# Channel mix by one level of Strassen's algorithm in a two-layer trunk: weight sums by accumulating DMAs, tiles in pools by phase

## The chip, the cores and the metric

The kernel runs on one core of a Trainium2 chip. A core has five engines with a queue each: TensorE (PE; its weight loads are listed apart as PEld), VectorE (DVE), ScalarE (ACT), GpSimd (POOL) and SyncE (SP), which here only issues DMAs. Each engine works through its own queue in order; semaphores tie the queues together. On-chip data lie in SBUF (128 partitions), products in PSUM (8 banks of 128 x 512 float32). The metric is the device time of one execution in microseconds.

## The reference

Two layers over 512 tokens with 1024 features. Cut to what matters (`i` is the layer):

```python
h = rmsnorm(x, norm1_g[i]);  z = h @ w_in[i] + b_in[i]
y_m = sigmoid(mo) * head_layernorm(mlstm(mq, mk, mv, mi, mf))        # 4 heads
y_r = silu(rg) * head_layernorm(retention(rq, rk, rv))               # 4 heads
merged = sigmoid(gm) * (y_m @ w_bm[i]) + sigmoid(gr) * (y_r @ w_br[i])
x = x + merged @ w_out[i]
h2 = rmsnorm(x, norm2_g[i])
x = x + square(relu(h2 @ w_ff1[i] + b_ff1[i])) @ w_ff2[i] + b_ff2[i]   # channel mix, 1024 -> 4096 -> 1024
h3 = rmsnorm(x, norm3_g[i])
x = x + sigmoid(h3 @ w_pe_gate[i]) * (p[i] @ w_pe[i])
return rmsnorm(x, final_g)
```

The change is in the fourth line from the end, the channel mix; it is 2 x 1024 x 4096 weights per layer.

## The kernel before

Activations lie transposed: features on partitions, the 512 tokens on the free axis. So a tile of weights (128 x 128) is the operand that PE holds, and the tokens stream past it. Every float32 operand of PE is split into two parts, `hi` = the value rounded to PE's float32r and `lo` = the rest; a product is the three matmuls hi*hi, hi*lo and lo*hi (`mm3`, lines 196 to 198). A split is two instructions: ACT writes `hi` by a copy, then DVE subtracts it and writes `lo`.

The weights come as one stream of 406 units of 512 KB (203 per layer) in the order of use. A unit of kind T8 holds the weights of 128 output features: 8 tiles for the 8 tiles of input features. `load_unit` issues a unit's DMA on SP's queue into `wr` (4 buffers) and splits it into `wh` (line 183, ACT) and `wl` (line 185, DVE), 3 buffers each; `unit` keeps two units ready beyond the one in use. `t8` then runs the unit's 24 matmuls of 512 tokens into one PSUM bank.

The channel mix takes the 4096 hidden features in four blocks `b` of 1024. For each block, eight `t8` make the hidden features (PSUM tiles `l0f`): DVE multiplies by the norm's reciprocal root, ACT adds the bias and takes the relu, POOL squares (line 747), and ACT and DVE split the result into `hid`. Then eight `t8` multiply `hid` by `w_ff2` (PSUM tiles `l0fo`), and DVE adds each into `x` (lines 777 and 779). The norm's sum of squares over features (`finish`) and the spreading of the reciprocal root over partitions (`spread`) are short matmuls after the first and the second `t8` of block 0; so the first result is held until then.

Ahead of the channel mix stand the out projection (`l0wo`, eight `t8`), which makes the norm's operand tile by tile (`n2.tile`), and behind it the layer's embedding (`l0pe`) and its gate (`l0pg`). At the very end of layer 1 the last four units of the gate are run in two halves of 256 tokens (PSUM tiles `pl`).

What sets the order: the code is written in the order of PE's work, and a scheduler orders each engine's queue from it by what is ready; pools hand out buffers, and a queue waits where a buffer is still read.

Of the kernel before, what the change touches and what calls it, by code (L numbers as in the profile page):

```python
# [22 lines left out]
P = 128  # L23
T = 512
# [6 lines left out]
UN = 1024  # L31
LOOK = 2
LAST = 4

# columns of w_in
# [3 lines left out]
# columns of the per-partition vectors  # L39
# [9 lines left out]

def unit_list():  # L50
    """What each unit of the weight stream holds, in the order of use (one layer)."""
# [48 lines left out]
    full("w_in", CGR)  # L100
# [11 lines left out]
    full("w_br", 0, 1024)  # L112
    full("w_out")
    for b in range(4):
        full("w_ff1", b * 1024)
        full("w_ff2", 0, b * 1024)
    u.append(("PE", 0))
    u.append(("PE", 1))
    full("w_pe_gate")
# [3 lines left out]
def build(ctx, tc, ins, out):  # L123
    nc = tc.nc
    ve, ac, gp, te = nc.vector, nc.scalar, nc.gpsimd, nc.tensor
    units = unit_list()
# [4 lines left out]

    cpool = pool("const", 1)
    wpool = pool("w", 3)
    apool = pool("act", 8)
    bpool = pool("big", 2)
    spool = pool("head", 4)
    tpool = pool("tmp", 7)
    opool = pool("one", 1)
    cols = pool("cols", 2)
    psum = pool("ps", 8, space=bass.MemoryType.PSUM)  # L140

    xs_dram = tc.dram_tile([KT, P, T], F32, name="x_spill")

# [10 lines left out]
    sel = cpool.tile([H, H, P], F32R, name="sel")  # L154
    cos = cpool.tile([P, T], F32, name="cos")
    sin = cpool.tile([P, T], F32, name="sin")
# [4 lines left out]
    def tmp(name, shape=(P, 516)):  # L161
        return tpool.tile(list(shape), F32, name=name, tag="t")

# [1 line left out]
    ready = []  # L165
    nxt = [0]

    def load_unit():
        n = nxt[0]
        if n >= L * NU:  # L170
            return
        nxt[0] += 1
        raw = wpool.tile([P, UN], F32, name=f"wr{n}", tag="wr", bufs=4)
        nc.sync.dma_start(raw, ins["wstream"][n])
        if n >= L * NU - LAST:
            hi = [apool.tile([P, T], F32R, name=f"wh{n}{a}", tag="Ah") for a in range(2)]
            lo = [apool.tile([P, T], F32R, name=f"wl{n}{a}", tag="Al") for a in range(2)]
            for a in range(2):
                split(raw[:, a * T:(a + 1) * T], hi[a], lo[a])
            ready.append((units[n % NU], hi, lo))  # L180
            return
        wh = wpool.tile([P, UN], F32R, name=f"wh{n}", tag="wh")
        ac.activation(wh, raw, AF.Copy)  # L183
        wl = wpool.tile([P, UN], F32R, name=f"wl{n}", tag="wl")
        ve.tensor_sub(wl, raw, wh.bitcast(F32))  # L185
        ready.append((units[n % NU], wh, wl))

    def unit(kind):
        while len(ready) < LOOK + 1 and nxt[0] < L * NU:
            load_unit()  # L190
        u, wh, wl = ready.pop(0)
        assert u[0] == kind, (u, kind)
        return u, wh, wl
# [6 lines left out]
    def t8(act, name):  # L200
        """One tile of columns against the 8 tiles of act: a PSUM tile [128 columns, tokens]."""
        _, wh, wl = unit("T8")
        o = ps(name)
        for k in range(KT):
            s = slice(k * P, (k + 1) * P)
            mm3(o, wh[:, s], wl[:, s], act[0][k], act[1][k], k == 0, k == KT - 1)
        return o

    def split(src, hi_ap, lo_ap):
        ac.activation(hi_ap, src, AF.Copy)  # L210
        ve.tensor_sub(lo_ap, src, hi_ap.bitcast(F32))

    def acts(side, name):
        hi, lo = [], []
        for k in range(KT):
            hi.append(apool.tile([P, T], F32R, name=f"{name}h{k}", tag=f"{side}h"))
            lo.append(apool.tile([P, T], F32R, name=f"{name}l{k}", tag=f"{side}l"))
        return hi, lo

# [1 line left out]
    class Norm:  # L221
        """Of the token tiles j0 .. j1 - 1."""

        def __init__(self, name, side, i, gain, j0=0, j1=NT):
# [3 lines left out]
            self.act = acts(side, name) if side else None  # L228
            self.sum = None
# [13 lines left out]

        def square(self, k, x, pool=False):
            w = self.n * P
            x = x[:, self.s]
            if self.sum is None:
                sq = opool.tile([P, T], F32, name=f"{self.name}sum", tag="bv" if self.s.start else "ssum")[:, :w]
            else:
                sq = tmp(f"{self.name}sq{k}")[:, :w]  # L250
# [24 lines left out]
        def spread(self):  # L275
            n = self.name
            w = self.n * P
            dh = opool.tile([P, 1280], F32R, name=f"{n}dh", tag="ph")[:, :w]
            dl = opool.tile([P, 1280], F32R, name=f"{n}dl", tag="pl")[:, :w]
# [7 lines left out]
            self.b = opool.tile([P, T], F32, name=f"{n}rb", tag="rb" if w == T else "dec")[:, :w]  # L287
# [6 lines left out]
    def rows_split_v(i, h, nm, n_, j, o, rc, bvt, vh, vl):  # L294
        """Token-major values of token tile j from the PSUM tile o: + bias, split, into vh, vl."""
# [15 lines left out]
    def values(i, nm, act, nrm, bv_ap, n_):  # L311
        bvt = opool.tile([P, T], F32, name=f"{nm}bv", tag="bv")
        nc.sync.dma_start(bvt, bv_ap)
        o = [ps(f"{nm}vp{j}") for j in range(NT)]
        for u in range(4):
            _, wh, wl = unit("V")
            for kk in range(2):
                k = 2 * u + kk
                s = slice(kk * T, (kk + 1) * T)
                for j in range(NT):  # L320
                    js = slice(j * P, (j + 1) * P)
                    te.matmul(o[j], act[0][k][:, js], wh[:, s], start=(k == 0), stop=False)
                    te.matmul(o[j], act[0][k][:, js], wl[:, s], start=False, stop=False)
                    te.matmul(o[j], act[1][k][:, js], wh[:, s], start=False, stop=(k == KT - 1))
        vh = [spool.tile([P, 516], F32R, name=f"{nm}vh{j}", tag="vh") for j in range(NT)]
        vl = [spool.tile([P, 516], F32R, name=f"{nm}vl{j}", tag="vl") for j in range(NT)]
# [4 lines left out]
    def scores(nm, qh, ql, kh, kl, decay):  # L331
        """P^T tiles: row tile i (128 keys), columns 128 i .. 511 (queries); times the decay."""
        ph = opool.tile([P, 1280], F32R, name=f"{nm}ph", tag="ph")
        pl = opool.tile([P, 1280], F32R, name=f"{nm}pl", tag="pl")
# [37 lines left out]
    def back(nm, num, v):  # L372
        """Columns tile v of the token-major heads, transposed: a PSUM tile [128 features, tokens]."""
# [103 lines left out]
    for i in range(L):  # L477
# [214 lines left out]
        for c in range(KT):  # L692
            gate_tile(sB, c, "bgr")
# [255 lines left out]
```

## Time and profile before

| | us |
|---|---|
| median of 3 runs (2438.12 to 2438.65) | 2438.5 |
| span of the profiled execution, first to last instruction | 2435.6 |
| PE busy | 2412.0 |
| DVE busy | 1349.9 |
| ACT busy | 928.9 |
| POOL busy | 231.0 |

The page gives no time of the profiled execution beside its span; the runs, which have no profile, are 2.9 us longer than the span (their median), which is what lies around the first and the last instruction. A row of a group reads: line, engine, operation, tile written <- tiles read, shapes, how many; after the bar the busy time in us and the mean duration of one in ns; after the second bar the idle time of the engine just before these instructions and what ended it. In a timeline the first two numbers are start and duration in us. Consecutive matmuls overlap in their durations, so their pace is read from starts.

### The profile page before, as it was taken

The numbers are of one execution on the slowest core, as the hardware profiler recorded it, in microseconds if no ns is written. First come the engines' busy times: TensorE is split into PE (matmuls) and PEld (weight loads), VectorE is DVE, ScalarE is ACT, GpSimd is POOL, SyncE is SP. The second block draws the span as 40 slices with busy tenths as digits, with TensorE's granted clock in tenths as the row PEclk, the third lists the DMA queues.
The fourth block names the chain that finished last, engine by engine and source line by source line (L and its number), as shares of the span: only waits on it lengthen the run. The fifth ranks groups of instructions, "written<-read, shape, count | busy, mean of one in ns | idle before, by whom it ended". The sixth has DMA issues, their size and how long they took to land.

```text
span 2435.6 us, 27773 instructions
## 1 busy us (share of the span) xinstructions
PE 2412.0 (99%) x11068; PEld 2006.5 (82%) x11068; DVE 1349.9 (55%) x1974; ACT 928.9 (38%) x1280; POOL 231.0 (9%) x277
## 2 busy tenths in 40 slices
PE   8999999999999999999999999999999999999997
PEld 6888888888888888888888888888888888888887
DVE  7867534666455434435578665446665554434445
ACT  3756323333233423324547552223323333223343
POOL 4000000000000201102101000000000011101122
PEclk9999999999999999999999999999999999999999
DMA  4222232322223333333322222322322242333331
GB/s 165 91 89 77 87 102 89 95 82 90 92 79 123 102 98 100 97 95 104 126 82 91 89 82 93 101 87 87 96 87 87 81 134 89 100 99 95 95 105 52
DMA packets 69498, 232.30 MB, mean 95 GB/s; under 512 B 7540, under 2 KB 9972, under 8 KB 69368
## 3 DMA queue, kind: packets, MB, share of 16 engines
q1 hardware_dynamic: 64040, 220.95, 29.1%
q10 hardware_dynamic: 5328, 9.57, 1.2%
q8 instruction: 87, 1.43, 0.2%
q14 instruction: 43, 0.35, 0.0%
HBM read 226.30 MB, written 4.19 MB: 95 GB/s over the span
## 4 chain that ended last, share of the span: by engine, by line
PE 98%; DVE 1%; ACT 0%; DVEq 0%; POOL 0%; issue 0%; ACTq 0%
PE l1f L196 2%; PE l1f L198 2%; PE l0f L198 2%; PE l1fo L198 2%; PE l0fo L198 2%; PE l0f L196 2%; PE l0fo L197 2%; PE l0f L197 2%; PE l1fo L197 2%; PE l1fo L196 2%; PE l1f L197 2%; PE l0fo L196 2%; PE l0br L196 1%; PE l1br L196 1%; PE l1br L197 1%; PE l0br L197 1%
## 5 line engine op out<-in xcount | busy, mean ns | idle before, releaser
L183 ACT ACTIVATE wh<-wr 128x1024 fp32r<-128x1024 f32 x402 | 426.4, 1061 | 1105.5 <-issue 210.2
L185 DVE TENSOR_TENSOR wl<-wr,wh 128x1024 fp32r<-128x1024 f32 x402 | 493.3, 1227 | 174.6 <-ACT wh L183 172.6
L196 PE MATMUL l1f<-l1n2h,wh 128*128 128x512 f32 x256 | 99.7, 389 | 0.0
L196 PE MATMUL l0f<-l0n2h,wh 128*128 128x512 f32 x256 | 99.7, 389 | 0.0
L198 PE MATMUL l0f<-l0n2h,wl 128*128 128x512 f32 x256 | 99.6, 389 | 0.0
L198 PE MATMUL l1f<-l1n2h,wl 128*128 128x512 f32 x256 | 99.6, 389 | 0.0
L197 PE MATMUL l0f<-l0n2l,wh 128*128 128x512 f32 x256 | 99.6, 389 | 0.0
L197 PE MATMUL l1f<-l1n2l,wh 128*128 128x512 f32 x256 | 99.6, 389 | 0.0
L747 POOL TENSOR_TENSOR l1ft<-l1ft 128x512 f32<-128x512 f32 x32 | 45.8, 1431 | 255.9 <-ACT l1ft L746 251.8
L747 POOL TENSOR_TENSOR l0ft<-l0ft 128x512 f32<-128x512 f32 x32 | 45.7, 1431 | 255.9 <-ACT l0ft L746 251.8
L197 PEld LDWEIGHTS l0f<-l0n2l,wh 128*128 128x128 f32 x256 | 48.1, 188 | 10.1
L197 PEld LDWEIGHTS l1f<-l1n2l,wh 128*128 128x128 f32 x256 | 48.1, 188 | 10.1
L198 PEld LDWEIGHTS l1f<-l1n2h,wl 128*128 128x128 f32 x256 | 48.1, 188 | 10.0
L198 PEld LDWEIGHTS l0f<-l0n2h,wl 128*128 128x128 f32 x256 | 48.0, 188 | 10.0
L196 PEld LDWEIGHTS l0f<-l0n2h,wh 128*128 128x128 f32 x256 | 48.1, 188 | 9.9
L196 PEld LDWEIGHTS l1f<-l1n2h,wh 128*128 128x128 f32 x256 | 48.1, 188 | 9.9
L779 DVE TENSOR_TENSOR l1x<-l1fo,l1x 128x512 f32<-128x512 f32 x24 | 16.6, 691 | 67.1 <-PE l1fo L198 67.1
L779 DVE TENSOR_TENSOR l0x<-l0fo,l0x 128x512 f32<-128x512 f32 x24 | 16.6, 691 | 66.0 <-PE l0fo L198 66.0
L745 DVE TENSOR_TENSOR l0ft<-l0f,l0n2rb 128x512 f32<-128x512 f32 x32 | 22.0, 691 | 35.7 <-PE l0f L198 35.7
L745 DVE TENSOR_TENSOR l1ft<-l1f,l1n2rb 128x512 f32<-128x512 f32 x32 | 22.0, 691 | 35.6 <-PE l1f L198 35.6
L711 DVE TENSOR_TENSOR l0brt<-l0br,l0sB 128x512 f32<-128x512 f32 x16 | 11.1, 692 | 36.2 <-PE l0br L198 36.2
L711 DVE TENSOR_TENSOR l1brt<-l1br,l1sB 128x512 f32<-128x512 f32 x16 | 11.1, 691 | 36.2 <-PE l1br L198 36.2
(2001 smaller groups left out, 6852.7 us busy)
## 6 DMA issues: line engine op xcount, KB each, us to landing
wr<-wstream SPq DMA_DIRECT2D x406, 512.0 KB, 3.5
x<-xT SPq DMA_DIRECT2D x4, 512.0 KB, 5.9
l0xr<-xT ACTq DMA_DIRECT2D x8, 256.0 KB, 2.5
x_spill<-l0x ACTq DMA_DIRECT2D x8, 256.0 KB, 2.8
l1xr<-x_spill ACTq DMA_DIRECT2D x8, 256.0 KB, 2.6
out<-l1x SPq DMA_DIRECT2D x4, 256.0 KB, 2.6
out<-l1x SPq DMA_DIRECT2D x2, 384.0 KB, 3.9
l0pt<-pT ACTq DMA_DIRECT2D x2, 256.0 KB, 2.7
```

The lines of the kernel that those rows point to most:

```text
L183: ac.activation(wh, raw, AF.Copy)
L185: ve.tensor_sub(wl, raw, wh.bitcast(F32))
L196: te.matmul(o, sh, mh, start=first, stop=False)
L197: te.matmul(o, sh, ml, start=False, stop=False)
L198: te.matmul(o, sl, mh, start=False, stop=last)
L711: ve.tensor_tensor(t[:, :T], o, sB[:, c, :], OP.mult)
L745: ve.tensor_tensor(t[:, :T], o, n2.b, OP.mult)
L747: gp.tensor_tensor(t[:, :T], t[:, :T], t[:, :T], OP.mult)
L779: ve.tensor_tensor(x[:, c, :], o, x[:, c, :], OP.add)
```

## The change

The channel mix is done by one level of Strassen's algorithm (in Winograd's form). Two `t8` units of 256 output features become one unit PAIR: a matrix of 1024 x 256 weights seen as 2 x 2 blocks, B11, B21, B22, B12, each 512 x 128 (256 KB); the tokens are seen as two halves of 256 and the input features as two halves of 512. Seven block products of 12 matmuls with 256 tokens (P1 to P7) take the place of 48 matmuls with 512 tokens. Four of the seven weight operands are sums of blocks. They are made in place: after the split of a raw block, POOL issues a DMA that adds the next block from memory to the raw buffer (`gp.dma_start(..., accum_op=OP.add)`), and the sum is split in turn: B11, then t1 = B11+B12, then t2 = t1+B22, then t4 = t2+B21 out of one buffer, and t3 = B22+B12 out of another. (The signs are put into the sums of the tokens and the evacuations.) On the other side, each pair of feature tiles has four quarters of 256 tokens and four sums of them, made by `pair_operand` (DVE) and split; there are seven operand columns `hi`, `lo` of 256.

All weights now come in blocks of 256 KB; a T8 unit is two of them, each loaded and split by itself (7 buffers of `wr`, `wh`, `wl`; `use` prepares 4 blocks ahead). The order of the 64 pairs (32 per layer) and their products is a list: per layer four pairs of `w_ff1`, then a pair of the next block, four pairs of `w_ff2`, three more of `w_ff1`, and so on; P4 of a pair comes after P1 of the next. The relu's square moves from POOL to ACT. The embedding's product stands ahead of the last four pairs. The gate `gr` is computed at the end of the second branch, the first half of the second branch's product goes to memory (`br_dram`) and back, and tiles live in pools that are opened and released by phase.

```diff
-        raw = wpool.tile([P, UN], F32, name=f"wr{n}", tag="wr", bufs=4)
-        nc.sync.dma_start(raw, ins["wstream"][n])
...
+PRODUCTS = {"P1": ("B11", 0), "P2": ("B21", 2), "P3": ("B22", 6), "P4": ("t4", 1), "P5": ("t1", 4),
+            "P6": ("t2", 5), "P7": ("t3", 3)}
+def pair_schedule(n):
...
+    for i in range(n):
+        out.append((i, "P1"))
+        if i:
+            out.append((i - 1, "P4"))
+        out += [(i, x) for x in ("P5", "P2", "P6", "P3", "P7")]
+def prep_schedule(n):
...
+    for i in range(n):
+        out += [(i, "B11"), (i, "B22")]
+        if i:
+            out.append((i - 1, "t4"))
+        out += [(i, x) for x in ("t1", "B21", "t2", "t3")]
...
+    def prep_next():
...
+        raw = raws[n, q]
+        split(raw, wh, wl)
+        pieces[n, x] = wh, wl
+        more = {"B11": 3, "B22": 3, "t1": 2, "t2": 1}.get(x)
+        if more is not None:
+            gp.dma_start(raw, block(n, more), accum_op=OP.add)
...
+        def product(self, x):
...
+            for k in range(4):
...
+                te.matmul(o, wh[:, s], h[:, m], start=f, stop=False, skip_group_check=True)
+                te.matmul(o, wh[:, s], l[:, m], start=False, stop=False, skip_group_check=True)
+                te.matmul(o, wl[:, s], h[:, m], start=False, stop=e, skip_group_check=True)
+            self.done(x, o)
+    def pair_operand(name, st, hi, lo):
+        ve.tensor_tensor(v[:, 4:6, :], v[:, 1:3, :], v[:, 0:1, :].to_broadcast([P, 2, S]), OP.subtract)
+        ve.scalar_tensor_tensor(v[:, 6, :], v[:, 5, :], -1.0, v[:, 1, :], OP.mult, OP.subtract)
+        ve.scalar_tensor_tensor(v[:, 7, :], v[:, 6, :], -1.0, v[:, 3, :], OP.mult, OP.subtract)
+        split(st[:, 4 * S:8 * S], hi[:, 3 * S:7 * S], lo[:, 3 * S:7 * S])
...
+                    if x_ in ("P1", "P5", "P6"):
+                        keep[x_] = small(nm + x_)
+                        ac.activation(keep[x_], o, AF.Copy)
+                    elif x_ == "P2":
+                        ve.tensor_tensor(v[:, 1, :], o, keep["P1"], OP.add)
+                        ve.tensor_tensor(v[:, 1, :], v[:, 1, :], n2.b[:, S:], OP.mult)
+                        act(1, 2, 0, 1.0)
+                    elif x_ == "P3":
+                        ve.tensor_tensor(v[:, 3, :], o, keep["P6"], OP.add)
+                    elif x_ == "P7":
+                        ve.tensor_tensor(v[:, 2, :], o, keep["P5"], OP.add)
+                        ve.tensor_tensor(st[:, 2 * S:4 * S], st[:, 2 * S:4 * S], n2.b, OP.mult)
+                        act(2, 4, 1, -1.0)
+                        pair_quarters(st, *hid[b, p])
+                    elif x_ == "P4":
+                        ve.tensor_tensor(v[:, 0, :], o, n2.b[:, :S], OP.mult)
+                        act(0, 1, 0, 1.0)
+                        pair_operand(nm, st, *hid[b, p])
```

Three places in the engines' queues. First, ACT in a stretch of `w_ff2` before: one split per `t8` and nothing else (`wh141` is the hi part of unit 141).

```order
L183 ACTIVATE wh139_6657<-wr139_6655 128x1024
L746 ACTIVATE l0ft07_6649<-l0ft07_6649,bc_85 128x512
L210 ACTIVATE l0h0h7_6329<-l0ft07_6649 128x512
L183 ACTIVATE wh140_6689<-wr140_6687 128x1024
L183 ACTIVATE wh141_6721<-wr141_6719 128x1024
```

And ACT in such a stretch now (`wh135_t2` is the hi part of t2 of pair 135, `wr135_0` the raw buffer in which B11, t1, t2, t4 of that pair are made one after the other):

```order
L225 ACTIVATE wh135_t2_8087<-wr135_0_7748 128x512
L225 ACTIVATE wh135_t3_8105<-wr135_2_7795 128x512
L225 ACTIVATE wh136_B11_8125<-wr136_0_7901 128x512
L225 ACTIVATE wh136_B22_8144<-wr136_2_7946 128x512
L225 ACTIVATE wh135_t4_8162<-wr135_0_7748 128x512
L225 ACTIVATE wh136_t1_8181<-wr136_0_7901 128x512
L225 ACTIVATE wh136_B21_8199<-wr136_1_7991 128x512
L225 ACTIVATE wh136_t2_8219<-wr136_0_7901 128x512
```

Seven splits of half the width stand there per pair, and those of t1, t2, t4 read a buffer that was split two to four places earlier in the same queue.

Second, DVE in a stretch of `w_ff1` now, from the subtraction for t2 of pair 133 to that for t1 of pair 134 (`l0f03st` and `l0f10st` are the staging tiles of two pairs' hidden features, `l0hl03` the lo part made from one):

```order
L226 TENSOR_TENSOR wl133_t2_7798<-wr133_0_7442,wh133_t2_7797 128x512
L945 TENSOR_TENSOR l0f10st_7775<-l0f10b_7848,l0f10P1_7793 128x256
L226 TENSOR_TENSOR l0hl03_7772<-l0f03st_7622,l0hh03_7771 128x768
L226 TENSOR_TENSOR wl133_t3_7823<-wr133_2_7489,wh133_t3_7822 128x512
L362 TENSOR_TENSOR l0f03st_7622<-l0f03st_7622 128x512
L226 TENSOR_TENSOR wl134_B11_7844<-wr134_0_7595,wh134_B11_7843 128x512
L363 SCALAR_TENSOR_TENSOR l0f03st_7622<-l0f03st_7622 128x256
L946 TENSOR_TENSOR l0f10st_7775<-l0f10st_7775,l0n2rb_7225 128x256
L364 SCALAR_TENSOR_TENSOR l0f03st_7622<-l0f03st_7622 128x256
L226 TENSOR_TENSOR wl134_B22_7866<-wr134_2_7642,wh134_B22_7865 128x512
L226 TENSOR_TENSOR wl133_t4_7885<-wr133_0_7442,wh133_t4_7884 128x512
```

Between the splits of two weight blocks stand the evacuations of products and the sums and splits of the hidden features; before, a stretch of `w_ff1` had one weight split, one multiplication and one split of 512 per `t8`.

Third, POOL, which before squared the hidden features:

```order
L747 TENSOR_TENSOR l0ft00_6421<-l0ft00_6421 128x512
L747 TENSOR_TENSOR l0ft01_6427<-l0ft01_6427 128x512
L747 TENSOR_TENSOR l0ft02_6464<-l0ft02_6464 128x512
```

and which now issues four accumulating DMAs per pair:

```order
L280 DMA wr135_0_7748<-wstream 128x512
L280 DMA wr135_2_7795<-wstream 128x512
L280 DMA wr135_0_7748<-wstream 128x512 x2
L280 DMA wr136_0_7901<-wstream 128x512
L280 DMA wr136_2_7946<-wstream 128x512
L280 DMA wr136_0_7901<-wstream 128x512 x2
```

The rows of one raw buffer (`wr135_0`) are the three additions of a pair that follow on one another; each waits for the DVE subtraction of the split before it.

More of the change, by code (lines that the diff above doesn't have):

```diff
@@ L111, in unit_list, with pairs @@
     rg(3)
-    full("w_br", 0, 1024)
+    for c in range(8):
+        t8("w_in", CGR + c * P)
+        t8("w_br", c * P, 1024)
     full("w_out")
-    for b in range(4):
-        full("w_ff1", b * 1024)
-        full("w_ff2", 0, b * 1024)
+    def pairs(seq):
+        for kind, b, p in seq:
+            if kind == "f":
+                u.append(("PAIR", "w_ff1", 0, b * 1024 + 256 * p))
+            else:
+                u.append(("PAIR", "w_ff2", b * 1024, 256 * p))
+    pairs(ff_order()[0])
     u.append(("PE", 0))
     u.append(("PE", 1))
+    pairs(ff_order()[1])
     full("w_pe_gate")
@@ L188, in unit, with tmp, split @@
-    def unit(kind):
[L189 to L193, printed above, removed]
+    def tmp(name, shape=(P, 516), dt=F32):
+        return cur["tmp"].tile(list(shape), dt, name=name, tag="t", bufs=cur["ntmp"])
+    def split(src, hi_ap, lo_ap):
+        ac.activation(hi_ap, src, AF.Copy)
+        ve.tensor_sub(lo_ap, src, hi_ap.bitcast(F32))
+    use_order, prep_order, loads = [], [], []
@@ new lines, in build, with block, load_next, fill_raws @@
+    first_block = np.cumsum([0] + [4 if u[0] == "PAIR" else 2 for u in units])
+    raws, pieces = {}, {}
+    at = {"use": 0, "prep": 0, "load": 0, "raw": 0}
+    def block(n, q):
+        return ins["wstream"][int(first_block[n]) + q]
+    def load_next():
+        n, q = loads[at["load"]]
+        at["load"] += 1
+        at["raw"] += 1
+        raws[n, q] = wpool.tile([P, Q], F32, name=f"wr{n}_{q}", tag="wr", bufs=RAWS)
+        nc.sync.dma_start(raws[n, q], block(n, q))
+    def fill_raws():
+        while at["load"] < len(loads) and at["raw"] < RAWS:
+            load_next()
@@ L247, in square @@
             if self.sum is None:
[L248 removed]
+                sq = opool.tile([P, T], F32, name=f"{self.name}sum", tag="ssum" + self.half)[:, :w]
             else:
```

429 lines of the change are left out of this document (280 added, 149 removed).

## The prediction

> **What bounds the kernel now.** I read the page's busy times and chain first, then who PE waits for, then the stage of the channel mix, then rows of single operations.
>
> ```profile
> PE 2412.0 (99%) x11068; PEld 2006.5 (82%) x11068; DVE 1349.9 (55%) x1974; ACT 928.9 (38%) x1280; POOL 231.0 (9%) x277
> ...
> PE 98%; DVE 1%; ACT 0%; DVEq 0%; POOL 0%; issue 0%; ACTq 0%
> ```
>
> PE is busy for 99% of the span and makes 98% of the chain that ends last. Two stretches, all ahead of the channel mix of layer 0 and that channel mix (columns: length, then busy PE, PEld, DVE, ACT, POOL, granted clock, DMA share, GB/s):
>
> ```profile
> 0.00:809.00 809.00, 798.93 (x3665) 662.26 (x3666) 489.91 (x748) 318.71 (x449) 58.81 (x110) 1.00 0.31 98
> 809.00:1159.00 350.00, 350.00 (x1554) 290.01 (x1553) 154.69 (x179) 118.50 (x147) 56.89 (x42) 1.00 0.31 98
> ```
>
> In the 350 us of the channel mix PE has no gap, and DVE and ACT are busy for 155 and 119 us of it: nobody makes PE wait. So time changes only by less PE work, or by a new wait of PE. PE's pace is read from starts: 192 matmuls of 512 tokens (first and last kind of one block), and 39 rows of 256 tokens from the end of layer 1.
>
> ```profile
> L196 PE MATMUL l0fo<-l0h0h,wh x64: 389/389/389, 854.8 to 897.6; 128*128 128x512 f32 x64
> ...
> L198 PE MATMUL l0fo<-l0h0h,wl x64: 389/389/389, 855.3 to 898.1; 128*128 128x512 f32 x64
> ```
>
> ```profile
> 2395.37 0.28 PE L196 MATMUL pl<-l1n3h,wh 128*128 128x256 f32 x1
> ...
> 2399.93 0.28 PE L198 MATMUL pl<-l1n3h,wl 128*128 128x256 f32 x1
> ```
>
> (898.1-854.8)/191 = 0.2267 us with 512 tokens; (2399.93-2395.37)/38 = 0.120 us with 256, more than half.
>
> **The PE work.** A pair is 48 matmuls before, 48 x 0.2267 = 10.88 us; now 7 x 12 = 84 of 256 tokens, 84 x 0.120 = 10.08 us. That is 0.80 us less, and 64 pairs give -51 us: Strassen's eighth (1.36 us per pair) loses 0.56 to the pace of short matmuls. The Trainium skill (TensorE: Matmul & The Clock Gate, section Back-to-back issue gap) gives N/2.4 + 2.5 ns, 109 ns with 256 tokens; by it the pair would be 9.2 us, but the rows say 120 ns, and they decide.
>
> **The other engines' work per pair.** Rows for durations:
>
> ```profile
> L210 ACT ACTIVATE wh<-wr 128x512 fp32r<-128x512 f32 x8 | 4.7, 622 | 1.3 <-DMA wr<-wstream 1.3
> L803 ACT ACTIVATE l1pgt<-l1pgt 128x256 f32<-128x256 f32 x8 | 3.3, 414 | 5.3 <-DVE l1pgt L802 5.3
> L746 ACT ACTIVATE l0ft<-l0ft,bc 128x512 f32<-128x512 f32 x32 | 22.6, 710 | 1.9 <-DVE l0ft L745 1.9
> L183 ACT ACTIVATE wh<-wr 128x1024 fp32r<-128x1024 f32 x402 | 426.4, 1061 | 1105.5 <-issue 210.2 <-PE l1fo L197 96.5 <-PE l0fo L197 96.5
> L211 DVE TENSOR_TENSOR wl<-wr,wh 128x512 fp32r<-128x512 f32 x8 | 5.2, 686 | 1.0 <-ACT wh L210 1.0
> L802 DVE TENSOR_TENSOR l1pgt<-pl,l1n3rb 128x256 f32<-128x256 f32 x8 | 3.4, 422 | 4.1 <-PE pl L198 3.9
> L185 DVE TENSOR_TENSOR wl<-wr,wh 128x1024 fp32r<-128x1024 f32 x402 | 493.3, 1227 | 174.6 <-ACT wh L183 172.6
> ```
>
> ```profile
> 11.65 0.61 ACT L254 ACTIVATE l0n1sq<-x 128x512 f32<-128x512 f32 x1
> 12.17 1.04 ACT L183 ACTIVATE wh<-wr 128x1024 fp32r<-128x1024 f32 x1
> ```
>
> The last two rows start 0.52 us apart while the first lasts 0.61: in a full queue an instruction costs 0.09 us less than its duration; I take that for DVE too. A `w_ff2` pair on DVE is 7 splits (0.69) and 7 additions of 256 (0.42): 7.8 us of durations, 6.5 packed. A `w_ff1` pair is 7 splits, 5 x 0.42 at the evacuations and 0.69 of 512, the 768 split (0.96, between the rows), and in `pair_operand` 0.69, 2 x 0.42 and 1.23: 18 instructions, 11.3 us, 9.7 packed. On ACT the latter is 7 x 0.62, 7 x 0.41, 0.71 and 0.62 of 512, 0.85 and 1.06: about 10.5, packed 8.8. So the slack of the stage before is gone in `w_ff1` pairs: DVE's packed work is nearly PE's 10.08.
>
> **The new wait: the chain of sums.** t1, t2, t4 of a pair come out of one buffer: split, addition by DMA, split, addition. Call L the time from the end of DVE's subtraction to the start of ACT's split of the summed buffer. No accumulating DMA and no DMA of POOL's is in the trace. Nearest rows (KB and us from issue to landing; then POOL's smallest work on 128 x 4 values):
>
> ```profile
> wr<-wstream SPq DMA_DIRECT2D x406, 512.0 KB, 3.5
> ...
> l0xr<-xT ACTq DMA_DIRECT2D x8, 256.0 KB, 2.5
> x_spill<-l0x ACTq DMA_DIRECT2D x8, 256.0 KB, 2.8
> ```
>
> ```profile
> L615 POOL TENSOR_TENSOR l0r1hv<-l0r1hv,nhalf 128x4 f32<-128x4 f32 x1 | 1.0, 1007 | 76.9 <-DVE l0r1hv L614 76.9
> ```
>
> Low end L = 2.5: as cheap as a plain 256 KB load. High end 1.0 + 3.5 = 4.5: POOL works 1 us on the issue, and because an addition reads the buffer besides memory it lands like 512 KB. I take 1.0 + 2.7 (the middle of the 256 KB rows is 2.65) = 3.7, since POOL's program makes this DMA and its least work is 1 us. A split from ACT's start to DVE's end is 0.62 + 0.69 + a hop of 0.04 = 1.35; the hop is read here (808.94 + 1.06 = 810.00):
>
> ```profile
> 808.94 1.06 ACT L183 ACTIVATE wh<-wr 128x1024 fp32r<-128x1024 f32 x1 [3.34 <-issue]
> ...
> 810.04 1.23 DVE L185 TENSOR_TENSOR wl<-wr,wh 128x1024 fp32r<-128x1024 f32 x1 [0.22 <-ACT wh L183]
> ```
>
> Now the order of the queues closes a loop. In a `w_ff2` stretch ACT splits t2, t3 of one pair, then B11 of the next. B11's subtraction ends 2 x 0.52 + 1.35 = 2.39 us after t2's split began; L later t1 can be split (t4, ready L after t2's subtraction, goes ahead of it, which fits); 1.35 + L after that t2 of the next pair. One turn is 3.74 + 2L, once per pair: 11.14 us at L = 3.7, against 10.08 of PE. In a `w_ff1` stretch DVE has five rows between t2's and B11's subtractions (the second place shown above the prediction): from 0.66 us on, 0.60, 0.33, 0.87, 0.60, 0.60, then 0.69 for B11: it ends 4.35 after t2's split began, and one turn is 5.70 + 2L = 13.1 us. ACT waiting there also holds the evacuations queued behind it; they fit into L. PE waits at P5 and P6, the users of t1 and t2; its queue holds everything else behind them. Four blocks prepared ahead are no help: the prepared blocks run dry in a loop slower than PE.
>
> Half of the pairs are of each kind: (11.14 + 13.1)/2 = 12.12, 1.24 more than the 10.88 of before; 64 pairs give +79 us. At L = 2.5 the loops are 8.7 (so PE's 10.08) and 10.7: mean 10.39, -31. At L = 4.5 they are 12.74 and 14.7: +182. The loops pay no longer where the mean is 10.88 less the 0.125 for the next term, at 5.70 + 2L = 11.43, L = 2.87.
>
> **The start of the channel mix.** Before, the first `t8` (5.44 us) covers the last operand tile. Now the last pair's operand needs, after the last out projection, on ACT and DVE in a row: 0.69 + 0.62 + 0.71, the 768 split 0.85, then on DVE 0.69, 0.42, 0.96, 0.42, the 1024 split 1.06 + 1.23, then `spread`'s eight small operations (128 x 128, about 0.2 each, an estimate: the line through the DVE rows of 256 and 512 gives 0.29, less 0.09): 9 us. PE has P1, P5 and three quarters of P6 (4 us) and the short matmuls of `finish` and `spread` (1.5 us) for it: about 4 us open, bounds 0 and 9; two layers +8.
>
> **Costed at nothing.** 278 units outside the channel mix are split in halves (ACT +0.18, DVE +0.15 us each, by 2 x 0.62 and 2 x 0.69 against 1.06 and 1.23, less 0.09 in the queue); 16 copies and 32 transfers of the spilled branch; a later gate; twice the DMAs on SP. Cover: PE's 799 us of the first stretch against 490 of DVE; without it DVE's part would be 40 us. POOL loses 64 squares of 1.43 us and gains 256 DMAs, four per pair: at 1 us each 4 of 12 us, so they queue little. The DMAs move 7/4 of the bytes of a stage whose share is 0.31. The end stays.
>
> **Sum.** +79 + 8 = +87. The profiled execution has a span of 2435.6, so 2523 there; its runs are 2.9 us longer at 2438.5, so 2526 us. From the bounds of L: 2415 to 2628.
>
> **Rivals.**
> 1. Faster: the addition costs no more than the plain 256 KB load, L = 2.5. Place: between the splits of t1 and t2; price -31 + 8 = 2415 us; decides below L = 2.87. For it: rows of 2.5 and 2.8. Against: they are of SP's and ACT's queues, without POOL, and read one operand. The Trainium skill (DMA: Bandwidth & Descriptors, section Anatomy of one DMA) fits a POOL-issued DMA by 2.0 us + bytes/436 GB/s, 2.6 us for 256 KB; no run here shows it, and it speaks for this rival (by it 2421 us).
> 2. Worse: the addition reads the buffer and POOL is late, L = 4.5 or more: 2628 us. For it: POOL and DVE slow each other in this trace; the same DVE row takes 1617 ns beside POOL's sums and 747 without:
>
> ```profile
> L242 DVE SCALAR_TENSOR_TENSOR l0n1l<-x,bc,l0n1h 128x512 fp32r<-128x512 f32 x8 | 12.4, 1617 | 0.0
> ...
> L242 DVE SCALAR_TENSOR_TENSOR l0n2l<-l0x,bc,l0n2h 128x512 fp32r<-128x512 f32 x8 | 6.0, 747 | 0.0
> ```
>
> Against: issuing a DMA touches little data.
> 3. No change: L is short, but DVE's instructions don't pack, as they wait for ACT by turns; `w_ff1` pairs go at DVE's 11.3, `w_ff2` pairs at 10.08: mean 10.69, -12 + 8: 2434 us. For it: DVE ended ACT's turns in the stage before too (the 172.6 us behind the row of `wl`). Against: it needs L below 2.87 too, as the loop is then the longer.
>
> **Chances.** Forecast (L of 3 to 4.5) 0.57; rival 1 0.16; rival 2 0.17; rival 3 0.10. The range goes from 2420, which leaves out about half of rival 1, to 2640, which leaves out two thirds of rival 2: together 2 in 10. Two runs of this kernel differ by less than 0.2% (5 us), so: faster 0.20 (rival 1 and 0.04 of rival 3), same 0.05 (of rival 3), slower 0.75. The likeliest case's own range: L of 3 to 4.5, 2447 to 2628.
>
> **What would show it.** Right: matmuls of the pairs start 0.12 us apart within a product; PE idles one to three us per pair, ended by the hi and lo parts of t1 and t2; ACT's splits `wh` wait for the DMA; the additions land well over 2.5 us after their issue; `w_ff1` stretches are longer than `w_ff2` ones by about 2 us per pair; PE idles some 4 us at the first pair of a layer. Wrong: landings below 2.5 us, or ACT waiting for POOL's transfer without PE waiting; or PE's pace in the products other than 0.12; or waits outside the channel mix, where I have none.

## The result, and the profile after

The changed kernel takes 2758.6 us (median of 4 runs, 2755.3 to 2761.7) against 2438.3 us (4 runs, 2438.1 to 2438.7): a ratio of 1.131 (95% interval 1.130 to 1.133), 320 us slower. The profiled execution has a span of 2753.6 us, 318 more than before. The page's busy times, and its row of the clock that TensorE was granted (40 slices of the span, in tenths):

```profile
PE 2505.1 (91%) x13372; PEld 2151.7 (78%) x13372; DVE 1666.9 (61%) x2961; ACT 1215.1 (44%) x2130; POOL 359.3 (13%) x469
...
PEclk9999999999999999998999999999999999998898
```

PE's share falls from 99% to 91%, and its busy time grows although a pair has less work: its clock is at one half in parts of the mixes (see the last step of the account below). Three stages (length, busy PE, PEld, DVE, ACT, POOL, granted clock, DMA share, GB/s): ahead of layer 0's channel mix, that mix, ahead of layer 1's.

```profile
0.00:825.60 825.60, 815.55 (x3664) 662.87 (x3665) 508.50 (x880) 354.56 (x595) 59.30 (x102) 1.00 0.35 100
825.60:1324.50 498.90, 389.12 (x2743) 364.07 (x2743) 295.34 (x537) 232.66 (x432) 118.43 (x132) 0.92 0.62 121
...
1374.00:2172.50 798.50, 798.50 (x3666) 661.50 (x3665) 491.33 (x869) 345.52 (x580) 34.61 (x74) 1.00 0.34 97
```

The same stages of the kernel before (its mix here with the embedding, which now stands inside the mix):

```profile
0.00:809.00 809.00, 798.93 (x3665) 662.26 (x3666) 489.91 (x748) 318.71 (x449) 58.81 (x110) 1.00 0.31 98
809.00:1172.40 363.40, 363.40 (x1621) 301.37 (x1620) 160.49 (x192) 125.93 (x159) 57.91 (x43) 1.00 0.31 97
1216.20:2010.00 793.80, 793.80 (x3666) 661.18 (x3665) 474.97 (x740) 312.39 (x439) 33.24 (x60) 1.00 0.30 92
```

The mix of layer 0 costs 135.5 us more, that of layer 1 145: 281 of the 318. The other 37 lie outside: 16.6 and 4.7 ahead of the two mixes, some 5 in the gate of layer 0, some 10 at the end. Inside layer 0's mix PE has 110 us without work. Summed from the trace, 55 of them end with the hi and lo parts of the summed operands (`wh_t`, `wl_t`), 27 with DVE's additions into `x` and 19 with the work of ACT and DVE on the hidden features. The last two stand in the same queues as the waiting splits. Some of PE's longest waits (us in total, times, longest):

```profile
PE l0f21a L340 <- ACT l0f21P L943: 3.5, 1, 3.5
...
PE l0o22a L340 <- DVE l0x L976: 2.9, 1, 2.9
...
PE l0f03c L340 <- ACT wh_t L225: 2.7, 1, 2.7
```

What the splits themselves wait for, by the page's groups:

```profile
L225 ACT ACTIVATE wh_t<-wr 128x512 fp32r<-128x512 f32 x256 | 157.7, 627 | 444.4 <-DMA wr<-wstream 412.4
L226 DVE TENSOR_TENSOR wl_t<-wr,wh_t 128x512 fp32r<-128x512 f32 x256 | 177.9, 704 | 279.2 <-ACT wh_t L225 278.5
L280 POOL DMA_DIRECT2D wr<-wstream x256 | 222.7, 876 | 782.4 <-DVE wl_t L226 340.9
...
wr<-wstream SPq DMA_DIRECT2D x748, 256.0 KB, 2.7
wr<-wstream POOLq DMA_DIRECT2D x256, 256.0 KB, 4.8
```

ACT's splits of the summed operands (`wh_t`) wait 412 us for the adding DMAs, over both layers. POOL is busy 0.88 us with each, and it lands 4.8 us after its issue; a plain load of the same 256 KB lands after 2.7. One link of the chain in the timeline (start, duration; t1 is split, POOL issues the addition that makes t2, t2 is split, PE goes on):

```profile
1056.35 0.63 ACT L225 ACTIVATE wh_t<-wr 128x512 fp32r<-128x512 f32 x1 [1.11 <-DVE l0x L976]
...
1057.01 0.69 DVE L226 TENSOR_TENSOR wl_t<-wr,wh_t 128x512 fp32r<-128x512 f32 x1 [0.72 <-ACT wh_t L225]
...
1058.06 0.86 POOL L280 DMA_DIRECT2D wr<-wstream  x1 [5.25 <-DVE wl_t L226]
...
1062.82 1.15 ACT L225 ACTIVATE wh_t<-wr 128x512 fp32r<-128x512 f32 x2 [5.32 <-DMA wr<-wstream]
...
1063.50 0.58 PE L340 MATMUL l0o12a<-l0hh,wh_t 128*128 128x256 f32 x1 [2.58 <-ACT wh_t L225]
```

From the end of the subtraction (1057.70) to ACT's split (1062.82) it is 5.12 us. That is the L of the prediction. Over the 64 pairs, with the rows of ACT and DVE matched to the program's order of splits, its median is 4.94 us for t1 and 5.26 for t2.

### The profile page after: what moved, and what is told of

The parts are those of the page before. It is cut to its first block, busy times and chain, and to the rows that moved or that the text cites. A ratio compares the mean times of both kernels' runs of the same rounds, so it can differ in the third digit from the quotient of the medians.

```text
span 2753.6 us, 36615 instructions
## 1 busy us (share of the span) xinstructions
PE 2505.1 (91%) x13372; PEld 2151.7 (78%) x13372; DVE 1666.9 (61%) x2961; ACT 1215.1 (44%) x2130; POOL 359.3 (13%) x469
## 5 line engine op out<-in xcount | busy, mean ns | idle before, releaser
L225 ACT ACTIVATE wh<-wr 128x512 fp32r<-128x512 f32 x556 | 347.8, 630 | 763.3 <-issue 78.8
L226 DVE TENSOR_TENSOR wl<-wr,wh 128x512 fp32r<-128x512 f32 x556 | 382.1, 692 | 356.5 <-ACT wh L225 352.2
L225 ACT ACTIVATE wh_t<-wr 128x512 fp32r<-128x512 f32 x256 | 157.7, 627 | 444.4 <-DMA wr<-wstream 412.4
L226 DVE TENSOR_TENSOR wl_t<-wr,wh_t 128x512 fp32r<-128x512 f32 x256 | 177.9, 704 | 279.2 <-ACT wh_t L225 278.5
L280 POOL DMA_DIRECT2D wr<-wstream x256 | 222.7, 876 | 782.4 <-DVE wl_t L226 340.9
L226 DVE TENSOR_TENSOR wl_B<-wr,wh_B 128x512 fp32r<-128x512 f32 x192 | 134.0, 700 | 13.3 <-ACT wh_B L225 10.3
L225 ACT ACTIVATE wh_B<-wr 128x512 fp32r<-128x512 f32 x192 | 113.6, 617 | 9.9 <-PE l1f00a L341 4.5
L299 PE MATMUL l0pg<-l0n3h,wh 128*128 128x512 f32 x64 | 25.8, 403 | 0.0
L300 PE MATMUL l0pg<-l0n3l,wh 128*128 128x512 f32 x64 | 25.6, 400 | 0.1
L301 PE MATMUL l0pg<-l0n3h,wl 128*128 128x512 f32 x64 | 25.5, 398 | 0.0
```

The source lines that it names most:

```text
L280: gp.dma_start(raw, block(n, more), accum_op=OP.add)
L299: te.matmul(o, sh, mh, start=first, stop=False)
L300: te.matmul(o, sh, ml, start=False, stop=False)
L301: te.matmul(o, sl, mh, start=False, stop=last)
```

## The experiments

Theory: PE's time in the mix is set by the loop through the splits and sums of t1 and t2, and L is longer than I took it. Rivals: bandwidth of the transfers, evacuations and PSUM banks, too small a stock of prepared blocks. Each run is one timed execution beside one of the kernel before on the same chip (2437.5 to 2438.4 us); the effects are far over the 0.2% that two runs differ by.

### The chain, taken away by degrees

```diff
 e1_plain
-            gp.dma_start(raw, block(n, more), accum_op=OP.add)
+            gp.dma_start(raw, block(n, more))
```

> POOL's four DMAs per pair become plain copies of the same block into the same buffer: the sums t1 to t4 are left out (each operand is the single block that came last), everything else stands, the waits too. Theory (the loop through t1 and t2 makes the pair's length, and an addition is late because it adds): the landing falls from 4.8 us after the issue to about 2.7, L from 5.1 to about 3.2 (0.36 + 0.86 + 2.0), the loops to 10.1 and 12.1 us, mean 11.1 against 14.9: 64 x 3.8 = 240 us less, about 2515 us. Rival (POOL's way of issuing is slow, whatever the DMA does): landing and time stay, 2740 to 2770 us.

Measured: 2590.7 us. First this run (POOL's queue with packets, MB and share of 16 engines; the issue; the landing), then that queue in the changed kernel:

```profile
q0 software_dynamic: 20480, 67.13, 8.8%
...
L280 POOL DMA_DIRECT2D wr<-wstream x256 | 138.6, 541 | 703.5 <-DVE wl_t L226 481.0
...
wr<-wstream POOLq DMA_DIRECT2D x256, 256.0 KB, 3.3
```

```profile
q0 software_dynamic: 36864, 67.13, 15.8%
```

Adding costs 0.34 us more on POOL and 1.5 us more to the landing, and 144 packets per transfer where a copy has 80. But a plain copy from POOL's queue still lands 0.6 us later than one from SP's. L is 3.99 and 3.50 here; the prediction's loops then are 3.74 + 7.49 and 5.70 + 7.49, mean 12.2, and 2758.6 - 64 x (14.9 - 12.2) = 2586, which is what was measured within 5 us. My 2515 came from too short an L again.

```diff
 e2_nochain
-        if x in (0, 1, "B11", "B21", "B22"):
-            loads.append((n, {"B11": 0, "B21": 1, "B22": 2}.get(x, x)))
+        loads.append((n, x))
...
-            gp.dma_start(raw, block(n, more), accum_op=OP.add)
...
```

> No chain: each of the seven operands of a pair gets a plain load of its own from SP's queue into a buffer of its own (t1 from the block B12, t2 from B22, t4 from B21, t3 from B12); the sums are left out, POOL issues no DMA, the bytes moved stay the same. Theory (chain of sums): PE no longer waits for t1 and t2, w_ff2 pairs go at PE's 10.1 us, w_ff1 pairs at 10.1 to 11.3 (DVE), the granted clock stays near 1.0 in the channel mix: 2758 - 64 x (14.9 - 10.4) = 2470, between 2430 and 2490 us; what is left over the 2387 of the PE work alone is the cost outside the pairs. Rival (DVE and ACT, or the reuse of PSUM banks by the seven products, hold PE): pairs stay at 13 us or more, over 2600 us. Rival (bandwidth of the transfers, 62% of 16 engines in this stage): the loads come late, landings over 4 us, over 2550 us.

Measured: 2443.3 us. The mix of layer 0, the embedding included, and PE's starts in its first product:

```profile
825.20:1171.60 346.40, 335.99 (x2743) 330.87 (x2742) 295.71 (x536) 233.30 (x430) 8.57 (x6) 0.99 0.58 174
```

```profile
825.23 0.28 PE L335 MATMUL l0f00a<-l0n2h,wh_B 128*128 128x256 f32 x1
825.35 0.28 PE L336 MATMUL l0f00a<-l0n2l,wh_B 128*128 128x256 f32 x1
```

It lasts 346 us in place of 499, with as many bytes moved, and PE's idle time in it falls from 110 to 10 us, that before evacuations too: bandwidth for these bytes, evacuations and banks by themselves don't make the loss. This run also takes away the adding and POOL's issuing; a run below with another order keeps both. Pairs follow at 9.9 to 10.0 us in the mean, and the mix of layer 0 is 17 us shorter than before; yet the whole is still 5 us slower than before. So even free sums win nothing while the 37 us outside stand.

```diff
 e3_ahead6
-AHEAD = 4
+AHEAD = 6
```

> Blocks are prepared six ahead of their use, not four. Theory (a loop slower than PE empties any stock): 2740 to 2775 us, no change. Rival (the stock of four is too small for a landing of 4.8 us): over 50 us faster.

Measured: 2739.3 us, 19 less, with the same waits:

```profile
L225 ACT ACTIVATE wh_t<-wr 128x512 fp32r<-128x512 f32 x256 | 156.4, 627 | 478.7 <-DMA wr<-wstream 433.6
```

A larger stock doesn't help a loop; the 19 us were not followed up.

### Sums made on chip by POOL

```diff
 e4_pooladd (a fourth raw block is loaded; 8 raw buffers in place of 7)
-            gp.dma_start(raw, block(n, more), accum_op=OP.add)
...
+        if x in ("B11", "t1", "t2"):
+            gp.tensor_tensor(raw, raw, raws[n, {"B11": 3, "t1": 2, "t2": 1}[x]], OP.add)
+        elif x == "B22":
+            gp.tensor_tensor(raws[n, 3], raws[n, 3], raw, OP.add)
...
```

> The four sums of a pair are made by POOL's own additions on chip (128 x 512, 1.43 us each in the trace of before, by its squares) of four plainly loaded blocks; no DMA adds. Theory: L = 1.43 + two hops, about 1.8 us; the loops are 3.74 + 3.6 = 7.3 and 5.70 + 3.6 = 9.3 us, under PE's 10.1; then DVE's w_ff1 pair (9.7 packed, 11.3 unpacked, longer if POOL slows DVE) is what is left: 2430 to 2520 us. Rival (the chain's length isn't what PE waits for): over 2650 us. Rival (POOL and DVE hinder each other so much that nothing is won): DVE rows of w_ff1 grow by half, 2550 to 2700 us.

Measured: 2581.3 us. POOL's additions and DVE's splits beside them, then 260 us of the mix:

```profile
L282 POOL TENSOR_TENSOR wr<-wr,wr 128x512 f32<-128x512 f32 x192 | 284.0, 1479 | 444.0 <-DVE wl_t L226 307.7
L226 DVE TENSOR_TENSOR wl_t<-wr,wh_t 128x512 fp32r<-128x512 f32 x256 | 245.0, 963 | 25.6 <-ACT wh_t L225 24.1
...
L226 DVE TENSOR_TENSOR wl_B<-wr,wh_B 128x512 fp32r<-128x512 f32 x192 | 207.8, 1088 | 19.9 <-ACT wh_B L225 19.3
```

```profile
850.00:1110.00 260.00, 221.92 (x1718) 214.68 (x1719) 249.04 (x339) 145.32 (x274) 128.95 (x82) 0.95 0.28 84
```

L fell to 2.1 and 1.5 us as expected, but the last rival came true: DVE's splits take 0.96 and 1.09 us beside POOL's additions (0.70 in the changed kernel), and DVE, busy 249 of 260 us, is near its limit. The Trainium skill (GPSIMD Engine Reference, section Specifications) says that the two share their ways into SBUF and contend where a DVE instruction has two inputs there; the rows agree.

```diff
 h4_mixed (as above for t1 and t2, with 7 raw buffers; t3 and t4 by DMA)
+        if x in ("B11", "t1"):
+            gp.tensor_tensor(raw, raw, raws[n, {"B11": 3, "t1": 2}[x]], OP.add)
+        if x == "B11":
+            gp.dma_start(raws[n, 3], block(n, 2), accum_op=OP.add)
+        elif x == "t2":
+            gp.dma_start(raw, block(n, 1), accum_op=OP.add)
...
```

> The changed kernel's order, with the two sums inside the loop (t1, t2) made by POOL's additions on chip and the two outside it (t3, t4) left to adding DMAs. Theory: L is 2.1 and 1.5 us, as measured with four sums on POOL, so the loops (7.3 and 9.3 us) don't bind; DVE loses half of the 3 us per pair that it lost there; pairs of 10.5 to 11.3: 2470 to 2530 us, faster than with four. Rival (POOL's queue: an addition stands behind a DMA's issue of 0.9 us and its wait, the chain is long again): 2580 us or more.

Measured: 2560.4 us, between the ranges of theory and rival: 21 us better than four sums on POOL, not the 50 to 110 expected. `wl_t` is back at 699 ns, `wl_B` still takes 1012. What takes the rest was not followed.

### The same sums in another order

```diff
 g1_skew6 (order of preparation in one period; 1 is the next pair, -1 the one before)
-  B11 B22 t4(-1) t1 B21 t2 t3
+  t1 B11(1) t3(-1) t4(-1) B22 t2 B21(1)
 order of use
-  P1 P4(-1) P5 P2 P6 P3 P7
+  P1 P5 P2 P7(-1) P4(-1) P6 P3
```

> The same blocks, sums and DMAs as in the changed kernel; only the order in which operands are prepared and used is another: B11 of the next pair is split ahead of t2 of this one, and the links of the chain stand 6, 5 and 5 places apart in the queue (in a period of seven). Theory (the loop is closed by the queue's order, not by L as such): three links in three periods, (3 x (5.1 + 1.35) + 5 x 1.1)/3 = 8.3 us per pair, under PE's 10.0; the pairs go at 10 to 11 us, as in the run without a chain: 2443 to 2510 us. Rival (bandwidth: at 10 us per pair the transfers would take 0.63 x 14.9/10 = 0.94 of the 16 engines, so landings grow until they bind again): landings over 6.5 us, pairs at 12 us or more, 2560 to 2680 us. Rival (it was not the order): 2740 us or more.

Measured: 2536.7 us, 222 less than the changed kernel with the same DMAs. Its transfers and 260 us of its mix:

```profile
wr<-wstream POOLq DMA_DIRECT2D x256, 256.0 KB, 5.2
```

```profile
850.00:1110.00 260.00, 241.37 (x1951) 235.67 (x1950) 202.56 (x379) 157.70 (x298) 80.28 (x93) 0.99 0.83 164
```

Landings are longer here (5.2 us, DMA share 0.83), and still the time falls: it was the queue's order that closed the loop. The theory's 2443 to 2510 was missed by 27 us.

```diff
 g2_skew4
+  preparation: t1 t4(-1) B22 B11(1) t2 B21 t3
+  use: P1 P5 P4(-1) P6 P2 P3 P7
```

> As before, with a smaller step: the links of the chain stand four places apart (B11 of the next pair three places ahead of t1's). Theory: (3 x 6.45 + 2 x 1.1)/2 = 10.8 us per pair, 14.9 before: about 2758 - 64 x 4.1 = 2500 us, 2480 to 2560, and slower than with the larger step if PE isn't the bound there. Rival (bandwidth): the same time as with the larger step, over 2560 us.

Measured: 2632.9 us. Less than a step of two to three places (2759), more than one of five to six (2537): the sign holds, the size doesn't, since 2480 to 2560 was forecast. The medians of L for t1 and t4 are 6.0 and 6.9 us here, as a sum that has landed also waits its turn in the queue; my formula leaves that out.

```diff
 i4_skew6_plain (g1_skew6 with)
-            gp.dma_start(raw, block(n, more), accum_op=OP.add)
+            gp.dma_start(raw, block(n, more))
```

> The run g1_skew6 with POOL's DMAs as plain copies (the sums are left out). It tells apart what still lies between that run (2537) and the one without a chain (2443). Theory (the adding transfers' landing and their share of the queues, 5.2 us and 0.84): landings of 3.3 us and a share under 0.65, pairs at PE's pace, 2445 to 2475 us. Rival (the new order of the products itself, with waits for evacuations): 2510 us or more.

Measured: 2469.4 us, landings of 3.1 us:

```profile
850.00:1110.00 260.00, 255.63 (x2105) 251.44 (x2105) 217.90 (x404) 170.18 (x319) 53.71 (x100) 0.99 0.60 178
```

So of the 93 us between g1_skew6 and the run without a chain, 67 belong to the adding transfers and 26 to the rest (2469 - 2443), in which the new order lies. The 315 us between the changed kernel and the run without a chain are thus 222 that the order alone gives back, 67 and 26.

```diff
 h1_one_row (g1_skew6 with the embedding as one place in a row of 32 pairs)
-        run_pairs([(ff1 if kind == "f" else ff2)(b, p) for kind, b, p in first])
+        run_pairs([(ff1 if kind == "f" else ff2)(b, p) for kind, b, p in first] + [embed]
+                  + [ff2(b, p) for _, b, p in rest], embed)
...
```

> The larger step of the run g1_skew6, and the embedding's eight products now stand inside one row of 32 pairs, where the row was cut in two (28 pairs, embedding, 4 pairs) and the chain of sums had to begin anew. Theory: from the last pair of w_ff1 (l0f33) to the end of the mix g1_skew6 took 85 us, the run without a chain 70.5: most of the 14 us per layer come back, 2505 to 2520 us. Rival (those 14 us are the wait for the last hidden features, not the chain): 2530 us or more.

Measured: 2537.4 us, no change: the 14 us per layer were not the chain's new start. PE's longest waits in that stretch are for DVE and ACT (columns: us in total, times, longest):

```profile
PE l0o32a L339 <- DVE l0x L978: 5.0, 1, 5.0
PE l0f32a L339 <- DVE l0f32st L953: 4.0, 1, 4.0
PE l0pe L298 <- ACT l0pth L218: 3.4, 1, 3.4
```

### The 37 us outside: where the operands lie

In the changed kernel the matmuls of 512 tokens ahead of layer 0's mix are slower, ahead of layer 1's partly, though PE waits no longer there than before. First and last kind of the product with `w_bm`:

```profile
L299 PE MATMUL l0bm<-l0ymh,wh x64: 392/395/396, 305.8 to 349.9; 128*128 128x512 f32 x64
...
L301 PE MATMUL l0bm<-l0ymh,wl x64: 392/395/396, 306.3 to 350.4; 128*128 128x512 f32 x64
```

(350.4 - 305.8)/191 = 0.2335 us, against 0.2267 before. The pools had moved the tiles, so I first asked whether it is the height in SBUF.

```diff
 g3_swap
-    xa_pool = phase("xa0", "right")
-    cur["low"] = phase("low0", "left")
+    xa_pool = phase("xa0", "left")
+    cur["low"] = phase("low0", "right")
...
-        act_side, ph_side = ("right", "left") if i == 0 else ("left", "right")
+        act_side, ph_side = ("left", "right") if i == 0 else ("right", "left")
```

> The pools change sides: in layer 0 the operands xa lie at 74 to 107 KB (197 to 229 KB in the changed kernel), in layer 1 the other way round. Theory (a matmul's pace goes with where its moving operand lies in SBUF: 227 ns low, 232 to 234 ns high): the 512 matmuls on xa go at 227 ns in layer 0 and at 232 to 234 in layer 1; the stretch ahead of layer 0's channel mix gets about 11 us shorter (825.6 to about 814), layer 1's (798.5) about 11 us longer; the whole time stays within 15 us. Rival (it goes with the layer or with what runs beside it): layer 0 keeps 825 us.

Measured: 2755.8 us; the stage ahead of layer 0's mix ends at 812.3 (825.6 in the changed kernel), that of layer 1 takes 811.4 (798.5). The slow pace goes with the place.

```diff
 g4_before_high (on the kernel before)
-    apool = pool("act", 8)
...
     cols = pool("cols", 2)
+    apool = pool("act", 8)
```

> The kernel before, with one line moved: the pool of the split operands is opened last and so lies at 163 to 228 KB in place of 55 to 121; head, tmp, one, cols move down by 64 KB. Nothing else. Theory (place in SBUF): its 512 matmuls go at 232 to 234 ns in place of 227, some 9000 of them: 40 to 60 us more, 2480 to 2500 us. Rival: 2438 us, no change.

Measured: 2496.5 us, 59 more from one moved line. That looked like height; but the move had also changed the addresses' remainders. Two controls:

```diff
 h2_before_shift (on the kernel before)
+    pool("pad", 1).tile([P, 24], F32, name="pad")
     apool = pool("act", 8)
 h3_before_high32 (on g4_before_high)
+    pool("pad", 1).tile([P, 8], F32, name="pad")
     apool = pool("act", 8)
```

> The kernel before with the pool of split operands moved up by 96 bytes only (an empty tile ahead of it): its tiles begin at a multiple of 128 bytes, as in g4_before_high, but stay at 55 to 121 KB. Theory (height in SBUF sets the pace): 2437 to 2441 us, 227 ns. Rival (the remainder by 128 bytes does it): 2480 us or more, 232 to 235 ns.

> g4_before_high with its operands moved up by another 32 bytes, so that they begin 32 bytes past a multiple of 128, as in the kernel before, but at 163 to 229 KB. Theory (height): 2490 to 2500 us, 232 to 235 ns. Rival (remainder): 2437 to 2441 us.

Measured: 2499.1 and 2437.9 us. The height theory falls twice: 96 bytes of shift at the same height cost 61 us, and 32 bytes at the great height give all 59 back. The products of `w_ff2`'s first block, shifted and then high with the old remainder:

```profile
L197 PE MATMUL l0fo<-l0h0h,wh x64: 392/392/392, 875.0 to 919.1; 128*128 128x512 f32 x64
...
L199 PE MATMUL l0fo<-l0h0h,wl x64: 399/399/399, 875.5 to 919.6; 128*128 128x512 f32 x64
```

```profile
L197 PE MATMUL l0fo<-l0h0h,wh x64: 389/389/389, 854.5 to 897.3; 128*128 128x512 f32 x64
...
L199 PE MATMUL l0fo<-l0h0h,wl x64: 389/389/389, 854.9 to 897.8; 128*128 128x512 f32 x64
```

(919.6 - 875.0)/191 = 0.2335 and (897.8 - 854.5)/191 = 0.2267. Sorting the matmuls of 512 tokens of these runs by the addresses of their two operands in the built programs gives a pattern: where the addresses have the same remainder by 256 bytes, the mean pace is 226.9 to 227.2 ns; where they differ by 32, 96, 128, 160 or 224, it is about 230 to 234. The large groups with equal remainders are the products with weights, with remainders of 160 (the kernel before) and 96 (the changed one); a few dozen matmuls of the heads with equal remainders of 0, 64 or 128 are at 231 ns and more, so it isn't shown that equality alone is enough. With 256 tokens it is 119.6 at the same remainder, 119.0 at 128 and 117 to 118 at 64. In the changed kernel some 4250 of the 6900 matmuls of 512 tokens have unequal remainders.

```diff
 i1_after_al
+    edge = phase("edge", "right")
+    edge.tile([P, 32], F32, name="edge")
...
-        return cur["tmp"].tile(list(shape), dt, name=name, tag="t", bufs=cur["ntmp"])
+        w = 576 if cur["tmp"] is cur["low"] else 516
+        return cur["tmp"].tile([P, w], dt, name=name, tag="t", bufs=cur["ntmp"])[:, 0:516]
...
```

> The changed kernel with small empty tiles between its pools and two tile widths rounded up (516 to 576 elements), so that the two operands of each matmul of 512 tokens begin at the same remainder by 256 bytes, and those of the pairs 64 bytes apart (the spacings with the shortest pace in the runs so far: 227 and 117 ns). Theory: about 4250 matmuls of 512 lose the 5.7 ns that they had gained (232.7 against 227): 24 us; the pairs are bound by the chain and stay: 2728 to 2742 us. Rival (the remainder matters in the kernel before only): 2750 us or more.

> The run e2_nochain (sums of the weights left out, plain loads) with the same placement. Theory: 24 us less outside the pairs, and, as PE is the bound in the pairs here, 0.1 to 0.2 us per pair: 2405 to 2420 us, under the 2438 of the kernel before; this is what the change would be worth with free sums and this placement. Rival (a wait elsewhere takes the gain): 2435 us or more.

> The run g1_skew6 (all sums made, the longer steps) with the same placement. Theory: 24 us outside the pairs and a few in them: 2500 to 2515 us. Rival (the transfers bind in the pairs and take back what is gained outside): 2515 to 2535.

Measured: 2735.2, 2413.4 and 2516.7 us. The first two are as forecast; the third gets 20 us back and lies 2 us over its range, where the rival stands. The changed kernel gets 23 us back, as the count of matmuls said, and the product with `w_bm` is at (344.4 - 301.1)/191 = 0.2267:

```profile
L300 PE MATMUL l0bm<-l0ymh,wh x64: 389/389/390, 301.1 to 343.9; 128*128 128x512 f32 x64
...
L302 PE MATMUL l0bm<-l0ymh,wl x64: 389/389/390, 301.5 to 344.4; 128*128 128x512 f32 x64
```

Without a chain the kernel is then 24.5 us faster than before (2437.9 beside it): that is what this change could be worth with free sums. With all sums made, the best of these versions is 2516.7 us; none that computes the reference beats the kernel before. By stages of the profiled executions, 26 of the 37 us outside come back in the changed kernel: the stages ahead of the mixes take 808.0 and 792.1 us (809.0 and 793.8 before). What remains lies in the gate of layer 0 and the end; these were not tried apart. The mixes together are 6 us longer than without the new placement.

## Why the prediction was right or wrong

The sign and the mechanism were right, the time (2526, range 2420 to 2640) was wrong. By its steps:

- **PE's work per pair** (10.08 us): right. Without the chain it is 9.94 in layer 0 (from 842.6 to 1101.1 us, 26 pairs), and the rows start 0.12 us apart. The Trainium skill's 109 ns that I set aside (TensorE: Matmul & The Clock Gate, section Back-to-back issue gap) is too short here, where the means are 117 to 120 ns at full clock.
- **The other engines' work per pair** (DVE's packed 9.7 us just fits): right. DVE's and ACT's work doesn't show in the run without a chain. Rival 3 falls.
- **The chain of sums**: this step failed, by the size of one term. The loops 3.74 + 2L and 5.70 + 2L hold nearly: their parts beside L measure 4.1 us in `w_ff2` pairs and 5.6 in `w_ff1` pairs (medians). The term L was mis-sized: I took 3.7 us, with 4.5 as the upper bound; it is 5.1. In the timeline above it is 0.36 us up to POOL's issue, which I had left out, 0.86 of issue, where I had 1.0, and 3.90 up to ACT's split, where I had 2.7. With the measured 4.94 + 5.26 they give 13.94 and 15.90 us, mean 14.9, and 64 x (14.9 - 10.9) = 259 us in place of the +79; the mixes lost 281, with the start. What failed is the bound from the nearest rows: plain transfers of 256 KB from ACT's queue and 512 KB from SP's price neither an addition (+1.5 us of landing) nor POOL's queue (3.3 us for a plain copy). Rival 2 ("L = 4.5 or more") was the case that came, and I gave it 0.17 and a price at its edge only. The 2 us by which `w_ff1` pairs should be longer than `w_ff2` pairs didn't come: from one split of t2 to the next, between pairs of one kind, it is 15.2 and 15.3 us (medians, the first pairs of a layer left out). L isn't the same in both: ahead of t1 it is 4.6 us in `w_ff1` and 5.3 in `w_ff2`, ahead of t2 5.2 and 5.4; why is not known.
- **"Four blocks prepared ahead are no help"**: right; six gave 19 us of 320.
- **The start of the channel mix** (+4 us per layer): too small. In the run without a chain the first pair takes 17.4 us up to the next P1, where six products of 1.44 are 8.6: some 9 us per layer, PE's half clock among it.
- **Costed at nothing**: wrong by 37 us. The cover that I named (PE's work over DVE's) holds ahead of the mixes, since PE doesn't wait longer there; it was PE's own pace that changed by where the pools put the operands. I had read that pace off one block and taken it for all; 26 of the 37 us are shown to be that. "The end stays" was wrong by some 10 us; its cause stays open.
- **The granted clock** was in no step. In the two mixes it is at one half in stretches of 3.4 us and multiples, 177 us in all (27 without a chain, none before). All of them begin on one grid of 3.41 us. In the two mixes, of the intervals of this grid that PE began at full clock, each of the 32 in which it idled 1.88 us or more is followed by one at half clock, and 8 of the 211 others are. So waits of 2 to 3 us are enough here. The Trainium skill (TensorE: Matmul & The Clock Gate, section Part 1: The HAM clock gate) puts it down to idle windows of about 3.4 us; the trace agrees in the length of the stretches, but just one of these 40 intervals was idle throughout. For layer 0's 2743 matmuls PE is busy 389 us, 336 without a chain: 53 of the 153 us between the two mixes are slower matmuls, 99 are idle time. Whether PE would have waited those 53 us anyway at full clock, no run here separates; no matmul is a part of the loop.

## What to carry to other kernels

A transfer that reads, adds and writes is another operation than a load: where the trace has none, its price has no upper bound in the rows of loads, and the range must say so. When engines work in order, ask of each chain how many of its links lie between two turns of the queue; spreading the links over more turns won 222 us here with the same transfers. Where a change makes PE wait often, look at the granted clock too: waits of 2 to 3 us came with half clock here. After tiles have been moved in SBUF, compare the pace of matmuls that wait for nothing before looking for waits.

## What was not expected of the hardware

- An adding DMA of 256 KB lands 4.8 us after its issue and takes 144 packets; a copy by the same queue 3.3 us and 80; a load from SP's queue 2.7. POOL is busy 0.88 and 0.54 us with the issue.
- The pace of matmuls depends on the two operands' addresses by 256 bytes: 227 ns against 230 to 234 with 512 tokens, 2.5% of a kernel that PE bounds (2437.9 and 2499.1 us). Why is not known from these runs.
- DVE's subtraction of two operands takes 0.96 to 1.09 us in the mean where POOL makes four additions per pair, 0.70 without.
- In the mixes of the changed kernel PE's clock was at one half after each interval of its 3.41 us grid in which PE had begun at full clock and idled 1.88 us or more (32 of 32); one interval was idle throughout.
